# A decoder block on one Trainium2 core: other banks and delays in the mix, score sums on GpSimd, three feature tiles first, and gate and up by seven block products

## The chip, the core and the metric

The kernel runs on one core of a Trainium2 chip. The core has five engines with a queue each: TensorE (PE, matmuls; PEld is its weight load), VectorE (DVE), ScalarE (ACT), GpSimd (POOL) and SyncE (SP, which here issues DMAs). The metric is the device time of one execution in microseconds (us), the median of the runs shown. The profile shows one execution.

## The reference

One decoder block, 512 tokens of 1024 channels, all float32. Cut to its steps:

```python
xn = rms_norm(h, mix_norm)
attn_cols, rwkv_cols, gate_cols = split(xn @ w_in)
# per 128 queries: 8 heads of index scores, the best 128 keys are kept, attention over these
scores = einsum('bqhs,bqh->bqs', relu(q_idx @ k_idx.T * 64**-0.5), w_idx) * 8**-0.5
y_attn = softmax(q @ k_sel.T * scale + bias) @ v_sel        # q, k with an RMS norm per head
y_rwkv = rwkv7_time_mix(rwkv_cols)                          # a recurrence over the 512 tokens
merged = sigmoid(g_a) * (y_attn @ w_branch_attn) + sigmoid(g_r) * (y_rwkv @ w_branch_rwkv)
h = h + merged @ w_out
hn = rms_norm(h, ffn_norm)
gate, up = split(hn @ w_gate_up)                            # 1024 -> 2 x 2816
h = h + (silu(gate) * up) @ w_down                          # 2816 -> 1024
```

## The kernel before, in words

Large products are made of three float32r matmuls each: an operand is split into a high part and what is left, the low part (names end in h and l, or `hi` and `lo`), and high x high, high x low and low x high are summed in PSUM. Weights come as a stream of 129 tiles of 128x1024 in the order of use. `chunk` fetches one: SP issues the DMA into `w_raw` (L236), ACT makes `w_hi` (L239), and POOL subtracts to `w_lo` (L243); from tile 17 on (`POOL_ONLY`) every third `w_lo` is DVE's. There are 2, 3 and 3 buffers of the three.

**The mix** (0 to about 518 us): the norm, the projections of `w_in`, index scores, the search for the best 128 keys, attention, the RWKV recurrence in chunks of 64 tokens, and the gates. `scores` takes query blocks 1 to 3, with 256, 384 and 512 keys. For each of 8 heads TensorE makes the product, ACT the relu (L425), and DVE one multiply-and-add into `score` (L426). `select` then finds the best keys with MAX8 and MATCH_REPLACE8 on DVE (L438, L439). `split_heads` writes the high and low parts of q and k; `kl` is subtracted on DVE (L459). `matrices` makes the 128x512 products that the recurrence needs, in PSUM banks of the kind "i" (2 banks; "d" and "c" have 3 each).

**TensorE's order** is the order of the program. `Streams` makes it: each part of the work is a generator that yields how long (by the planner's own clock) it is to rest, and among those that are due the one with the lowest rank goes on; `products`, with all large matrix products, has the last rank and fills up. The rests are in the table `L` (L89). The order on the other engines is the scheduler's.

**After the mix**: `w_out` in matmuls of 256 columns (518 to 567), the second norm with its transposes (`norm`, L317 to L338: ACT squares, POOL `ss`, DVE `xs`, flips on TensorE, `hnh` on ACT, `hnl` on DVE), then **gate/up** in 22 feature tiles of 128: weights 128x128 of gate, then of up, are stationary and 512 tokens move, 2 x 8 x 3 = 48 matmuls. The first tile runs in halves of 256 tokens (`dense_halves`), so that it can begin before the last tokens are normalized. ACT makes the silu (L1096), DVE multiplies (L1097), ACT and POOL split the result into `uh` and `ul` (L1100, L1101), which stay in SBUF. **Down** goes twice over the 22 tiles, for 512 output channels each, in matmuls of 512 columns: 528 of them.

Of the kernel before, what the change touches and what calls it, by code (L numbers as in the profile page):

```python
# [127 lines left out]
def hybrid_block(ctx: ExitStack, tc: tile.TileContext, x, first, rows, consts, lora, rel_bias, stream, out):  # L128
# [324 lines left out]
    def split_heads(j, src, gain, hi, lo, twice):  # L453

        for e in range(2):
            a, b, h = slice(64 * e, 64 * e + 64), slice(64 - 64 * e, 128 - 64 * e), 2 * j + e
            if gain is None:
                nc.scalar.activation(hi[a, h], src[a], AF.Copy)
                nc.vector.tensor_sub(lo[b, h], src[a], hi[a, h])  # L459
            else:  # L460
# [285 lines left out]
    def matrices():  # L746
        yield "prep"
        for t in range(NT):
            if t > 1:
                yield f"inv{t - 2}"  # L750
                yield f"step{t - 2}"
            l16 = l16s[t % 2]
            for e in range(2):
# [226 lines left out]
    def products(wt, w2):  # L980
# [106 lines left out]
        for j in range(NF):
            wg, wu = w_tile(128), w_tile(128)
            ps, pu = bank("d"), bank("d")
            if j == 0:  # L1090
# [6 lines left out]
            nc.vector.tensor_mul(g, pu, g)  # L1097
            uh = fp.tile([128, S], F32R, name="uh", tag="uh", bufs=NF)
            ul = fp.tile([128, S], F32R, name="ul", tag="ul", bufs=NF)
            nc.scalar.activation(uh, g, AF.Copy)  # L1100
            nc.gpsimd.tensor_sub(ul, g, uh)  # L1101
            up.append((uh, ul))
# [110 lines left out]
```

## Time and profile before

| | |
|---|---|
| time, median of 3 runs | 939.4 us (937.67 to 939.57) |
| the profiled execution, its own time | 937.07 us |
| its span on the core | 934.9 us, so 2.2 us lie around it |
| TensorE busy | 97% of the span |
| DVE, ACT, POOL busy | 44%, 37%, 39% |
| mix; w_out and norm; gate/up; down | to about 518; to 576; 576 to 811; 811 to 931 us |
| HBM | 74.5 MB read, 82 GB/s over the span |

The page of the profile gives busy times of the whole span, which mix stages of different kinds, so the stages are read apart: from the waits of TensorE, from windows, and from the starts of single instructions. A matmul's recorded length is longer than its share of the pipeline; its price is the distance between the starts of successive ones. Some matmul records are missing, so counts may fall short by a few per cent.

### The profile page before, as it was taken

The numbers are of one execution on the slowest core, as the hardware profiler recorded it, in microseconds if no ns is written. First come the engines' busy times: TensorE is split into PE (matmuls) and PEld (weight loads), VectorE is DVE, ScalarE is ACT, GpSimd is POOL, SyncE is SP. The second block draws the span as 40 slices with busy tenths as digits, with TensorE's granted clock in tenths as the row PEclk, the third lists the DMA queues.
The fourth block names the chain that finished last, engine by engine and source line by source line (L and its number), as shares of the span: only waits on it lengthen the run. The fifth ranks groups of instructions, "written<-read, shape, count | busy, mean of one in ns | idle before, by whom it ended". The sixth has DMA issues, their size and how long they took to land.

```text
span 934.9 us, 13570 instructions
## 1 busy us (share of the span) xinstructions
PE 906.9 (97%) x5526; PEld 763.2 (82%) x5526; DVE 412.5 (44%) x796; ACT 344.0 (37%) x548; POOL 363.7 (39%) x242
## 2 busy tenths in 40 slices
PE   7999988999999999999999999999999999999998
PEld 5978986888687787878888998888888888888886
DVE  4399998874686457666334435111111111110111
ACT  5464665554543333333243225223222322311220
POOL 6425631313374344253236522544444353433321
PEclk9999999999999999999999999999999999999999
DMA  6312332111221110010432321333333323322431
GB/s 234 95 56 68 109 98 69 32 37 57 68 83 54 64 50 24 24 43 28 135 103 81 111 91 55 104 107 94 93 90 102 102 90 111 92 90 90 152 97 45
DMA packets 24173, 77.77 MB, mean 83 GB/s; under 512 B 2869, under 2 KB 4366, under 8 KB 24112
## 3 DMA queue, kind: packets, MB, share of 16 engines
q1 hardware_dynamic: 20688, 72.49, 24.8%
q10 hardware_dynamic: 3424, 4.43, 1.6%
q8 instruction: 43, 0.70, 0.3%
q14 instruction: 18, 0.15, 0.1%
HBM read 74.53 MB, written 2.38 MB: 82 GB/s over the span
## 4 chain that ended last, share of the span: by engine, by line
PE 84%; DVE 11%; issue 2%; ACT 2%; POOL 1%; DMA 1%; SPq 0%; DVEq 0%; ACTq 0%; POOLq 0%
PE ps_d L162 60%; PE ps_c L162 11%; PE ps_i L162 9%; DVE score L439 2%; DVE max L438 2%; PE ps_c L169 2%; DVE kl L459 1%; POOL w_lo L243 1%; DMA xa<-in_x_dram 1%; DVE score L426 1%; DVE lg L569 0%; PE ps_i L169 0%; DVE w_lo L243 0%; ACT lg L576 0%; PE ps_d L169 0%
## 5 line engine op out<-in xcount | busy, mean ns | idle before, releaser
L243 POOL TENSOR_TENSOR w_lo<-w_raw,w_hi 128x1024 fp32r<-128x1024 f32 (+1 forms) x94 | 223.5, 2379 | 355.0 <-ACT w_hi L239 328.8
L239 ACT ACTIVATE w_hi<-w_raw 128x1024 fp32r<-128x1024 f32 x129 | 136.7, 1060 | 351.6 <-PE ps_d L162 216.7
L162 PE MATMUL ps_d<-xnl,w_hi 128*128 128x512 f32 (+2 forms) x360 | 141.8, 394 | 0.0
L162 PE MATMUL ps_d<-xnh,w_hi 128*128 128x512 f32 (+2 forms) x360 | 141.4, 393 | 0.0
L162 PE MATMUL ps_d<-xnh,w_lo 128*128 128x512 f32 (+2 forms) x360 | 141.0, 392 | 0.0
L162 PE MATMUL ps_d<-hnl,w_hi 128*128 128x512 f32 (+1 forms) x368 | 139.9, 380 | 0.4 <-DVE hnl L338 0.4
L162 PE MATMUL ps_d<-hnh,w_hi 128*128 128x512 f32 (+1 forms) x368 | 139.8, 380 | 0.0
L162 PE MATMUL ps_d<-hnh,w_lo 128*128 128x512 f32 (+1 forms) x368 | 139.8, 380 | 0.0
L243 DVE TENSOR_TENSOR w_lo<-w_raw,w_hi 128x1024 fp32r<-128x1024 f32 x37 | 47.5, 1283 | 127.2 <-ACT w_hi L239 126.7
L1097 DVE TENSOR_TENSOR gsig<-ps_d,gsig 128x512 f32<-128x512 f32 x22 | 15.2, 692 | 157.6 <-PE ps_d L162 156.9
L162 PEld LDWEIGHTS ps_d<-hnl,w_hi 128*128 128x128 f32 x368 | 69.2, 188 | 13.8 <-DVE hnl L338 0.6
L162 PEld LDWEIGHTS ps_d<-hnh,w_lo 128*128 128x128 f32 x368 | 69.2, 188 | 13.1
L162 PEld LDWEIGHTS ps_d<-hnh,w_hi 128*128 128x128 f32 x368 | 69.2, 188 | 13.0
L162 PEld LDWEIGHTS ps_d<-xnh,w_hi 128*128 128x128 f32 x360 | 68.7, 191 | 11.7 <-issue 1.0
L162 PEld LDWEIGHTS ps_d<-xnl,w_hi 128*128 128x128 f32 x360 | 68.8, 191 | 11.2 <-issue 1.8
L162 PEld LDWEIGHTS ps_d<-xnh,w_lo 128*128 128x128 f32 x360 | 68.7, 191 | 11.2 <-issue 1.4
L1101 POOL TENSOR_TENSOR ul<-gsig,uh 128x512 fp32r<-128x512 f32 x22 | 31.5, 1433 | 25.3 <-ACT uh L1100 14.4
L162 PE MATMUL ps_d<-w_hi,mh 128*128 128x256 f32 x120 | 34.0, 284 | 0.0
L162 PE MATMUL ps_d<-w_hi,ml 128*128 128x256 f32 x120 | 34.0, 283 | 0.0
L162 PE MATMUL ps_d<-w_lo,mh 128*128 128x256 f32 x120 | 34.0, 283 | 0.0
L576 ACT ACTIVATE lg<-lg,mx,qrs 128x128 f32<-128x128 f32 (+3 forms) x32 | 20.8, 650 | 22.7 <-DVE mx L575 22.7
L438 DVE MAX8 max<-score 128x8 f32<-128x256 f32 (+2 forms) x48 | 26.7, 559 | 1.0
(291 smaller groups left out, 1685.7 us busy)
## 6 DMA issues: line engine op xcount, KB each, us to landing
w_raw<-in_stream_dram SPq DMA_DIRECT2D x129, 512.0 KB, 3.6
xa<-in_x_dram SPq DMA_DIRECT2D x4, 512.0 KB, 5.8
ht<-in_x_dram ACTq DMA_DIRECT2D x8, 256.0 KB, 5.9
out_dram<-ht SPq DMA_DIRECT2D x8, 256.0 KB, 2.1
toep<-bias_table ACTq DMA_DIRECT2D x8, 128.0 KB, 2.8
gain<-in_rows_dram ACTq DMA_DIRECT2D x2, 256.0 KB, 4.4
con<-in_consts_dram SPq DMA_DIRECT2D x1, 321.0 KB, 6.8
bias_table<-tab ACTq DMA_DIRECT2D x1, 276.0 KB
```

What stands on the lines that cost most here:

```text
L162: nc.tensor.matmul(o, w, r, **kw)
L169: nc.tensor.transpose(o, src, idn)
L239: nc.scalar.activation(hi, raw, AF.Copy)
L243: eng.tensor_sub(lo[:, o:o + n_], raw[:, o:o + n_], hi[:, o:o + n_])
L426: nc.vector.scalar_tensor_tensor(sc, r, w, sc, op0=OP.mult, op1=OP.add)
L438: nc.vector.max(m8, sc)
L439: nc.vector.match_replace(sc, m8, sc, TAKEN)
L459: nc.vector.tensor_sub(lo[b, h], src[a], hi[a, h])
L576: nc.scalar.activation(lg, lg, AF.Exp, scale=scale, bias=mx[:, 2:3], accum_out=den[:, h:h + 1])
L1097: nc.vector.tensor_mul(g, pu, g)
L1101: nc.gpsimd.tensor_sub(ul, g, uh)
```

## The change

**In the table of rests**: `score` from 0.4 to 0.6, `rms` 6.5 to 9.0, `attn` (0.9, 0.9, 0.95, 1.0) to (1.3, 1.1, 1.0, 1.0), with 0.7 more after the first two heads of a query block, `inv_u` 3.25 to 4.2. `matrices` takes its banks from the kind "d".

**Scores**: heads 0 to 4 stay as they are. Heads 5 to 7 are weighted and summed on POOL, and DVE adds that sum once per block. `kl` of `split_heads` goes to POOL.

**Three feature tiles first**: the first gate, the first up and the second gate weight tile run in the halves.

**Gate and up by seven products**: from the third feature tile on, the 2x2 blocks are gate and up by the two halves of the 1024 input channels (a11, a12, a21, a22) on the one side, and the two halves of channels by two halves of the tokens on the other (b11 and so on, and their differences t1 to t4). Winograd's form of Strassen's algorithm needs seven block products instead of eight, each 4 x 3 matmuls of 256 columns. `seven_sides` makes t1 to t4 once, from `hnh` + `hnl`. Each tile's s1 to s4 are made of the raw weights on DVE, and seven operands are split: high parts on ACT, low parts on DVE, except those of a12 and a22 on POOL. The product's result stays whole (`u`), and down splits it into `us` at use, in each of its two passes, on ACT and DVE.

```diff
-L = dict(norm=3.0, normed=1.3, score=0.4, pick=0.15, rms=6.5, sums=4.0, attn=(0.9, 0.9, 0.95, 1.0), attn_out=2.0, sig=0.3,
-         prep=5.0, oper=6.0, bonus=9.0, mat=0.5, mats=2.8, inv_u=3.25, inv_t=1.4, inv_r=1.4, inv_n=0.9, inv_e=1.8,
+L = dict(norm=3.0, normed=1.3, score=0.6, pick=0.15, rms=9.0, sums=4.0, attn=(1.3, 1.1, 1.0, 1.0), attn_new=0.7, attn_out=2.0, sig=0.3,
+         prep=5.0, oper=6.0, bonus=9.0, mat=0.5, mats=2.8, inv_u=4.2, inv_t=1.4, inv_r=1.4, inv_n=0.9, inv_e=1.8,
...
-                    nc.vector.scalar_tensor_tensor(sc, r, w, sc, op0=OP.mult, op1=OP.add)
+                    if h < 5:
+                        nc.vector.scalar_tensor_tensor(sc, r, w, sc, op0=OP.mult, op1=OP.add)
+                    else:
+                        nc.gpsimd.tensor_scalar(r, r, w, None, op0=OP.mult)
+                        if h > 5:
+                            nc.gpsimd.tensor_add(r, r, more)
+                        more = r
                 yield L["score"]
+            nc.vector.tensor_add(sc, sc, more)
...
-                nc.vector.tensor_sub(lo[b, h], src[a], hi[a, h])
+                nc.gpsimd.tensor_sub(lo[b, h], src[a], hi[a, h])
...
-            yield L["attn"][i]
+            yield L["attn"][i] + (L["attn_new"] if u < len(units) and units[u][1] < 2 else 0.0)
...
-                    ps = bank("i").rearrange("q (h t) -> q h t", h=4)
+                    ps = bank("d").rearrange("q (h t) -> q h t", h=4)
...
-                yield from dense_halves([(ps, wg), (pu, wu)], hn, "hn")
+                outs = [(bank("d"), w_tile(128)) for _ in range(3)]
+                yield from dense_halves(outs, hn, "hn")
+                (ps, _), (pu, _), (ps_1, _) = outs
+                quads = seven_sides(fp, four_k, hn_)
...
+        def product(ps, hi, lo, b, first):
+            for k in range(4):
+                ks = slice(k * 128, k * 128 + 128)
+                xh, xl = b[k]
+                mm(ps, hi[:, ks], xh, start=first and k == 0, stop=False, skip_group_check=True)
+                mm(ps, hi[:, ks], xl, start=False, stop=False, skip_group_check=True)
+                mm(ps, lo[:, ks], xh, start=False, stop=k == 3, skip_group_check=True)
+
+        for j in range(2, NF):
...
+            a11, a12, a21, a22 = wg[:, 0:512], wg[:, 512:1024], wu[:, 0:512], wu[:, 512:1024]
+            s1, s2, s3, s4 = [unit("s") for _ in range(4)]
+            nc.vector.tensor_add(s1, a21, a22)
+            nc.vector.tensor_sub(s2, s1, a11)
+            nc.vector.tensor_sub(s3, a11, a21)
+            nc.vector.tensor_sub(s4, a12, s2)
...
+            w11, ws2 = two(a11, nc.vector, s2, nc.vector)
+            w12, ws3 = two(a12, nc.gpsimd, s3, nc.vector)
+            ws1, w22 = two(s1, nc.vector, a22, nc.gpsimd)
...
+            product(pa, *w11, b11, True)
+            nc.scalar.activation(u2, pa, AF.Copy)
+            yield 0.0
+            product(pb, *ws2, t2, True)
+            nc.vector.tensor_add(u2, pb, u2)
+            yield 0.0
+            product(pa, *w12, b21, False)
+            nc.scalar.activation(g[:, 0:256], pa, AF.Silu)
+            yield 0.0
+            product(pc_, *ws3, t3, True)
+            nc.vector.tensor_add(u3, pc_, u2)
+            yield 0.0
+            product(pd, *ws1, t1, True)
+            nc.vector.tensor_add(u3, pd, u3)
+            yield 0.0
+            product(pc_, *w22, t4, False)
+            nc.vector.tensor_add(c21, pc_, u2)
+            yield 0.0
+            product(pd, *ws4, b22, False)
+            nc.vector.tensor_add(u2, pd, u2)
+            nc.scalar.activation(g[:, 256:512], u2, AF.Silu)
+            u = up_rows(j)
+            nc.vector.tensor_mul(u[:, 0:256], g[:, 0:256], c21)
+            nc.vector.tensor_mul(u[:, 256:512], g[:, 256:512], u3)
...
+                for k in range(2):
+                    s = fp.tile([128, 2, S], F32R, name="us", tag="fx", bufs=3)
+                    nc.scalar.activation(s[:, 0], up[k0 // 2][:, k], AF.Copy)
+                    nc.vector.tensor_sub(s[:, 1], up[k0 // 2][:, k], s[:, 0])
+                    uu.append(s)
```

In `seven_sides` a difference is two 512 subtractions (`tf`), a high part `th` on ACT and a low part `tl` on DVE, each 128x1024:

```diff
+            nc.vector.tensor_add(f[q], a[0][q // 2][:, s], a[1][q // 2][:, s])
...
+        d1, t1 = minus(block(0, 1), block(0, 0))
+        d2, t2 = minus(block(1, 1), d1)
+        _, t3 = minus(block(1, 1), block(0, 1))
+        _, t4 = minus(block(1, 0), d2)
```

What the scheduler makes of it is seen in three places. In the gate/up loop DVE had two kinds of instructions, multiplications and some of the `w_lo`:

```order
L243 TENSOR_TENSOR w_lo<-w_raw,w_hi 128x1024
L1097 TENSOR_TENSOR gsig<-ps_d,gsig 128x512 x2
L243 TENSOR_TENSOR w_lo<-w_raw,w_hi 128x1024
L1097 TENSOR_TENSOR gsig<-ps_d,gsig 128x512
L243 TENSOR_TENSOR w_lo<-w_raw,w_hi 128x1024
```

Now a tile has 16, of which these are the first twelve from the sum behind the second product on (L1137 to L1140 are s1 to s4 of the next tile, L1144 are low parts, the others are sums with PSUM):

```order
L1164 TENSOR_TENSOR post<-ps_d,post 128x256
L1144 TENSOR_TENSOR w_lo<-w_raw,w_hi 128x512
L1137 TENSOR_TENSOR s<-wu_raw 128x512
L1138 TENSOR_TENSOR s<-s,w_raw 128x512
L1139 TENSOR_TENSOR s<-w_raw,wu_raw 128x512
L1170 TENSOR_TENSOR post<-ps_c,post 128x256
L1140 TENSOR_TENSOR s<-w_raw,s 128x512
L1144 TENSOR_TENSOR w_lo<-s,w_hi 128x512
L1173 TENSOR_TENSOR post<-ps_i,post 128x256
L1144 TENSOR_TENSOR w_lo<-s,w_hi 128x512
L1144 TENSOR_TENSOR s4l<-s,s4h 128x512
L1176 TENSOR_TENSOR upt<-ps_c,post 128x256
```

The weights of the next tile are prepared between the sums of the running one. On DVE behind the last `hnl` stood a `w_lo` and the first multiplications; now `seven_sides` stands there (`hnf` is `hnh` + `hnl`, `tf` and `tl` belong to t1 to t4):

```order
L338 TENSOR_TENSOR hnl<-ps_c,hnh 128x4x128 x2
L1214 TENSOR_TENSOR hnf<-hnh,hnl 128x1024 x4
L1223 TENSOR_TENSOR tf<-hnf 128x512 x2
L1223 TENSOR_TENSOR tf<-hnf,tf 128x512
L1223 TENSOR_TENSOR tf<-hnf 128x512 x2
L1223 TENSOR_TENSOR tf<-hnf,tf 128x512 x2
L243 TENSOR_TENSOR w_lo<-w_raw,w_hi 128x1024
L1226 TENSOR_TENSOR tl<-tf,th 128x1024
L1223 TENSOR_TENSOR tf<-hnf,tf 128x512
L1115 TENSOR_TENSOR u<-ps_d,gsig 128x512
L1226 TENSOR_TENSOR tl<-tf,th 128x1024
L1144 TENSOR_TENSOR w_lo<-w_raw,w_hi 128x512
```

The sides of the products stand ahead of the fourth weight tile's multiplication and of the first low parts of the third feature tile. On POOL during the scores, before and then now (`relu` holds a head's weighted score):

```order
L243 TENSOR_TENSOR w_lo<-w_raw,w_hi 128x1024 x10
L486 TENSOR_TENSOR qrs<-qss,half 128x32
L243 TENSOR_TENSOR w_lo<-w_raw,w_hi 128x1024
L502 TENSOR_TENSOR qrs<-qss,half 128x8
L243 TENSOR_TENSOR w_lo<-w_raw,w_hi 128x1024
```

```order
L243 TENSOR_TENSOR w_lo<-w_raw,w_hi 128x1024 x6
L430 TENSOR_SCALAR relu<-relu,widx 128x256 x3
L432 TENSOR_TENSOR relu<-relu 128x256 x2
L243 TENSOR_TENSOR w_lo<-w_raw,w_hi 128x1024
L430 TENSOR_SCALAR relu<-relu,widx 128x384 x2
L243 TENSOR_TENSOR w_lo<-w_raw,w_hi 128x1024
L432 TENSOR_TENSOR relu<-relu 128x384
L430 TENSOR_SCALAR relu<-relu,widx 128x384
L432 TENSOR_TENSOR relu<-relu 128x384
L430 TENSOR_SCALAR relu<-relu,widx 128x512 x3
L432 TENSOR_TENSOR relu<-relu 128x512
L243 TENSOR_TENSOR w_lo<-w_raw,w_hi 128x1024
```

The four last `w_lo` of that row of ten now stand among the weighted scores and their sums.

## Rows read from the trace of the kernel before

**Rows 1.** The page's first part: busy time, share of the span and instructions of each engine.

```profile
PE 906.9 (97%) x5526; PEld 763.2 (82%) x5526; DVE 412.5 (44%) x796; ACT 344.0 (37%) x548; POOL 363.7 (39%) x242
```

**Rows 2.** TensorE's waits over the whole span: the waiting line, what it waited for, us in total, times, the longest.

```profile
PE ps_c L169 <- ACT lg L576: 6.2, 6, 2.3
...
PE ps_i L169 <- ACT ksq L503: 2.2, 1, 2.2
PE ps_c L162 <- DVE score L422: 1.9, 1, 1.9
PE ps_i L162 <- DVE uu L816: 1.8, 2, 1.1
PE ps_i L162 <- ACT tt L813: 1.6, 2, 1.1
PE ps_c L169 <- DVE xs L330: 1.2, 1, 1.2
```

**Rows 3.** Windows: from:to, length, busy time (and instructions) of PE, PEld, DVE, ACT, POOL, the granted clock of TensorE as a share of full speed, the DMA share, GB/s.

```profile
60.00:70.00 10.00, 8.10 (x29) 6.18 (x28) 9.76 (x21) 5.16 (x9) 3.07 (x2) 0.83 0.15 52
130.00:150.00 20.00, 17.41 (x101) 14.49 (x100) 19.02 (x48) 9.22 (x21) 4.77 (x2) 0.91 0.26 80
...
600.00:780.00 180.00, 180.00 (x796) 149.05 (x795) 25.24 (x28) 52.77 (x68) 75.41 (x39) 1.00 0.32 97
811.00:931.00 120.00, 120.00 (x530) 99.07 (x528) 12.89 (x14) 21.79 (x21) 34.74 (x15) 1.00 0.30 93
```

**Rows 4.** The timeline of TensorE in `w_out` (256 columns, the first and the last of 28 in a row) and in gate/up (512 columns, the first and the last of 10): start, recorded length, instruction.

```profile
529.74 0.28 PE L162 MATMUL ps_d<-w_hi,ml 128*128 128x256 f32 x1
...
532.98 0.28 PE L162 MATMUL ps_d<-w_hi,ml 128*128 128x256 f32 x1
...
595.41 0.39 PE L162 MATMUL ps_d<-hnh,w_lo 128*128 128x512 f32 x1
...
597.45 0.39 PE L162 MATMUL ps_d<-hnh,w_lo 128*128 128x512 f32 x1
```

**Rows 5.** The timeline of DVE and POOL where instructions of both meet, and once where POOL's is alone (803.83): start, length, instruction, idle time before it and its releaser.

```profile
120.73 2.23 DVE L459 TENSOR_TENSOR kl<-kraw,kh 64x512 fp32r<-64x512 f32 x1
...
120.06 2.35 POOL L243 TENSOR_TENSOR w_lo<-w_raw,w_hi 128x1024 fp32r<-128x1024 f32 x1 [0.28 <-ACT w_hi L239]
...
503.35 1.67 POOL L1067 TENSOR_TENSOR gr<-gr,mrg 128x512 f32<-128x512 f32 x1 [1.43 <-DVE gr L973]
...
503.79 2.31 DVE L243 TENSOR_TENSOR w_lo<-w_raw,w_hi 128x1024 fp32r<-128x1024 f32 x1
...
506.63 0.68 DVE L1069 SCALAR_TENSOR_TENSOR ml<-gr,mh 128x512 fp32r<-128x512 f32 x1
...
569.82 2.39 POOL L243 TENSOR_TENSOR w_lo<-w_raw,w_hi 128x1024 fp32r<-128x1024 f32 x1
...
570.71 1.29 DVE L338 TENSOR_TENSOR hnl<-ps_c,hnh 128x512 fp32r<-128x512 f32 x2 [0.83 <-ACT hnh L337]
...
594.71 1.23 DVE L243 TENSOR_TENSOR w_lo<-w_raw,w_hi 128x1024 fp32r<-128x1024 f32 x1 [0.15 <-ACT w_hi L239]
...
595.30 1.78 POOL L1101 TENSOR_TENSOR ul<-gsig,uh 128x512 fp32r<-128x512 f32 x1 [3.59 <-ACT uh L1100]
...
803.83 1.27 POOL L1101 TENSOR_TENSOR ul<-gsig,uh 128x512 fp32r<-128x512 f32 x1
```

**Rows 6.** Groups of instructions by line and form, from 567 to 931 us, and of the whole span for the 256 form of `ht`: busy time, mean ns of one, idle time before them and its releaser.

```profile
L243 DVE TENSOR_TENSOR w_lo<-w_raw,w_hi 128x1024 fp32r<-128x1024 f32 x21 | 25.7, 1225 | 116.7 <-ACT w_hi L239 116.2
...
L338 DVE TENSOR_TENSOR hnl<-ps_c,hnh 128x512 fp32r<-128x512 f32 x6 | 4.0, 688 | 1.6 <-ACT hnh L337 1.5
...
L1077 DVE TENSOR_TENSOR ht<-ps_d,ht 128x256 f32<-128x256 f32 x15 | 5.8, 420 | 18.9 <-PE ps_d L162 18.9
...
L243 POOL TENSOR_TENSOR w_lo<-w_raw,w_hi 128x1024 fp32r<-128x1024 f32 x44 | 105.3, 2393 | 190.6 <-ACT w_hi L239 190.6
...
L239 ACT ACTIVATE w_hi<-w_raw 128x1024 fp32r<-128x1024 f32 x65 | 68.9, 1061 | 249.1 <-PE ps_d L162 138.9 <-PE ps_i L162 82.9 <-issue 27.3
L1100 ACT ACTIVATE uh<-gsig 128x512 fp32r<-128x512 f32 x22 | 13.9, 632 | 0.0
L1096 ACT ACTIVATE gsig<-ps_d 128x512 f32<-128x512 f32 x22 | 12.8, 583 | 0.0
```

**Rows 7.** The timeline of DVE at the start of gate/up: the last two `hnl` and the first multiplication.

```profile
574.88 1.42 DVE L338 TENSOR_TENSOR hnl<-ps_c,hnh 128x512 fp32r<-128x512 f32 x2 [0.71 <-ACT hnh L337]
...
582.96 0.69 DVE L1097 TENSOR_TENSOR gsig<-ps_d,gsig 128x512 f32<-128x512 f32 x1 [0.70 <-ACT gsig L1096]
```

**Rows 8.** Groups by line and form: DVE from 40 to 150 us, and a POOL group of the whole span.

```profile
L459 DVE TENSOR_TENSOR kl<-kraw,kh 64x512 fp32r<-64x512 f32 x8 | 7.5, 933 | 0.2
...
L426 DVE SCALAR_TENSOR_TENSOR score<-relu,widx,score 128x384 f32<-128x384 f32 x7 | 5.8, 824 | 0.0
L426 DVE SCALAR_TENSOR_TENSOR score<-relu,widx,score 128x512 f32<-128x512 f32 x7 | 5.5, 782 | 0.0
...
L426 DVE SCALAR_TENSOR_TENSOR score<-relu,widx,score 128x256 f32<-128x256 f32 x7 | 4.1, 584 | 1.0 <-DVE score L426 0.5
...
L859 POOL TENSOR_TENSOR kbs<-kb,pchunk 128x512 f32<-128x512 f32 x7 | 7.3, 1037 | 0.4
```

More of the change, by code (lines that the diff above doesn't have):

```diff
@@ L33 @@
 UNITS, WBUFS = {"ua": 10, "uc": 8}, (2, 3, 3)
-UA = ("score", "relu", "widx_t", "tab", "ytile", "sg", "ag", "wa2", "seg", "am", "u32", "ht")
+UA = ("score", "relu", "widx_t", "tab", "ytile", "sg", "ag", "wa2", "seg", "am", "u32", "ht", "upt")
 SMALL = {"ss": 4, "max8": 3, "mx": 4}
@@ L1085, in products, with up_rows @@
         fp = ctx.enter_context(tc.tile_pool(name="ffn", bufs=1))
+        four_k = lambda name, tag, n: fp.tile([128, 4, 256], F32R if tag == "tx" else F32, name=name, tag=tag, bufs=n)
+        tags = ["d", "c", "i", "d", "c", "d", "c", "i"]
         up = []
-        for j in range(NF):
-            wg, wu = w_tile(128), w_tile(128)
-            ps, pu = bank("d"), bank("d")
+        def up_rows(j):
+            if j % 2 == 0:
+                up.append(fp.tile([128, 2, S], F32, name="u", tag="u", bufs=NF // 2))
+            return up[j // 2][:, j % 2]
@@ L1090, in products @@
+        for j in range(2):
             if j == 0:
-                yield from dense_halves([(ps, wg), (pu, wu)], hn, "hn")
-            else:
-                yield from dense_t(ps, wg, slice(0, 128), hn)
-                yield from dense_t(pu, wu, slice(0, 128), hn)
+                outs = [(bank("d"), w_tile(128)) for _ in range(3)]
+                yield from dense_halves(outs, hn, "hn")
+                (ps, _), (pu, _), (ps_1, _) = outs
+                quads = seven_sides(fp, four_k, hn_)
+            else:
+                ps, pu = ps_1, bank("d")
+                yield from dense_t(pu, w_tile(128), slice(0, 128), hn)
@@ L1095, in products @@
             g = unit("gsig")
             nc.scalar.activation(g, ps, AF.Silu)
[L1097 to L1102, printed above, removed]
+            nc.vector.tensor_mul(up_rows(j), pu, g)
+        b11, b21, b22, t1, t2, t3, t4 = quads
+        def product(ps, hi, lo, b, first):
[5 more added lines that the diff above has]
+                mm(ps, lo[:, ks], xh, start=False, stop=k == 3, skip_group_check=True)
@@ new lines, in products, with split, two @@
+        for j in range(2, NF):
+            wg = wp.tile([128, 1024], F32, name="w_raw", tag="w_raw", bufs=WBUFS[0])
+            wu = fp.tile([128, 1024], F32, name="wu_raw", tag="fx", bufs=3)
+            for w in (wg, wu):
+                nc.sync.dma_start(w, stream[at[0]])
+                at[0] += 1
+            a11, a12, a21, a22 = wg[:, 0:512], wg[:, 512:1024], wu[:, 0:512], wu[:, 512:1024]
[4 more added lines that the diff above has]
+            nc.vector.tensor_sub(s4, a12, s2)
+            def split(h, l, w, eng):
+                nc.scalar.activation(h, w, AF.Copy)
+                eng.tensor_sub(l, w, h)
+                return h, l
+            def two(wa, ea, wb, eb):
+                h = wp.tile([128, 1024], F32R, name="w_hi", tag="w_hi", bufs=WBUFS[1])
+                l = wp.tile([128, 1024], F32R, name="w_lo", tag="w_lo", bufs=WBUFS[2])
+                return split(h[:, 0:512], l[:, 0:512], wa, ea), split(h[:, 512:1024], l[:, 512:1024], wb, eb)
+            w11, ws2 = two(a11, nc.vector, s2, nc.vector)
+            w12, ws3 = two(a12, nc.gpsimd, s3, nc.vector)
+            ws1, w22 = two(s1, nc.vector, a22, nc.gpsimd)
+            ws4 = split(fp.tile([128, 512], F32R, name="s4h", tag="s4h", bufs=2),
+                        fp.tile([128, 512], F32R, name="s4l", tag="s4l", bufs=2), s4, nc.vector)
+            pa, pb, pc_, pd = [bank(tags[(4 * j + i) % 8])[:, 0:256] for i in range(4)]
+            post, upt, g = unit("post"), unit("upt"), unit("gsig")
+            u2, u3, c21 = post[:, 0:256], post[:, 256:512], upt[:, 0:256]
+            product(pa, *w11, b11, True)
[22 more added lines that the diff above has]
+            nc.vector.tensor_mul(u[:, 256:512], g[:, 256:512], u3)
@@ L1108, in products @@
                 wt = chunk(2, 512)
+                uu = []
+                for k in range(2):
[3 more added lines that the diff above has]
+                    uu.append(s)
                 last = k0 == NF - 2
@@ L1112, in products @@
                     j, ts = k0 + k, slice(t * 128, t * 128 + 128)
-                    uh, ul = up[j][0][:, ts], up[j][1][:, ts]
+                    uh, ul = uu[k][:, 0, ts], uu[k][:, 1, ts]
                     mm(pss[t], uh, wt[k][0], start=(j == 0), stop=False)
@@ L1119, in products, with seven_sides, block, minus @@
                         nc.sync.dma_start(out[t * 128:(t + 1) * 128, cs], ht[t][g])
+    def seven_sides(fp, four_k, a):
+        f = []
+        for q in range(4):
+            f.append(fp.tile([128, 2, S], F32, name="hnf", tag="u", bufs=NF // 2))
+            s = slice(2 * (q % 2), 2 * (q % 2) + 2)
+            nc.vector.tensor_add(f[q], a[0][q // 2][:, s], a[1][q // 2][:, s])
+        def block(k, t):
+            return [f[2 * k + e][:, :, 256 * t:256 * t + 256] for e in range(2)]
+        def minus(x, y):
+            d = four_k("tf", "u", NF // 2)
+            r = [d[:, 2 * e:2 * e + 2] for e in range(2)]
+            for e in range(2):
+                nc.vector.tensor_sub(r[e], x[e], y[e])
+            h, l = four_k("th", "tx", 8), four_k("tl", "tx", 8)
+            nc.scalar.activation(h, d, AF.Copy)
+            nc.vector.tensor_sub(l, d, h)
+            return r, [(h[:, k], l[:, k]) for k in range(4)]
+        d1, t1 = minus(block(0, 1), block(0, 0))
+        d2, t2 = minus(block(1, 1), d1)
+        _, t3 = minus(block(1, 1), block(0, 1))
+        _, t4 = minus(block(1, 0), d2)
+        as_is = lambda k, t: [(a[0][k][:, i, 256 * t:256 * t + 256], a[1][k][:, i, 256 * t:256 * t + 256])
+                              for i in range(4)]
+        return as_is(0, 0), as_is(1, 0), as_is(1, 1), t1, t2, t3, t4
     st.add(2, bias_table(), 30.0)
```

## The prediction

> **What bounds the kernel now.** I read the page's busy times first [rows 1]: TensorE is busy 97% of the span, so the time is what TensorE executes plus some thirty microseconds in which it waits or runs at a lower clock. Then TensorE's waits [rows 2]: nearly all lie in the mix, the longest sum (6.2 us) behind the softmax's `lg`, and in gate/up and down there is none but the 1.2 us for the last norm. So gate/up shortens only if TensorE gets fewer or shorter instructions, and the mix only by its waits. The windows [rows 3] add the clock: it is 0.83 in 60:70 and 0.91 in 130:150, 1.00 in gate/up and down.
>
> The price of a matmul is read from the starts of successive ones [rows 4]: at 256 columns 27 steps take 3.24 us, 120.0 ns each; at 512 columns 9 steps take 2.04 us, 226.7 ns each. Both kinds load new weights every time. Half the columns cost 53%, not 50%.
>
> **Gate/up on TensorE.** A feature tile took 2 x 8 x 3 = 48 matmuls of 512 columns: 10.88 us. With seven block products it takes 7 x 4 x 3 = 84 of 256: 10.08 us. That is -0.80 us for each of 20 tiles, **-16.0 us**. The third and fourth weight tile in the norm's halves: only one more (24 matmuls of 512, 5.44 us, become 48 of 256, 5.76 us), **+0.3 us**. The norm's 1.2 us wait stays, since the flips and what POOL has queued before `ss` are the same.
>
> Both prices lie 13.3 ns above the columns at 2.4 GHz (106.7 and 213.3 ns), and that fixed part takes a third of what fewer columns would give (84 x 106.7 against 48 x 213.3 ns would be -1.28 a tile). The Trainium skill ("TensorE: Matmul & The Clock Gate", section "Back-to-back issue gap") gives columns / 2.4 GHz plus about 2.5 ns. By that, 84 x 109.2 ns against 48 x 215.8 ns would be -1.2 us a tile and -24 us in all, and the sum 916 instead of 924. The trace does not agree (it shows 120.0 and 226.7), and the rows decide.
>
> **What the loop asks of DVE.** This is the term that decides. Gate/up now gives DVE 25.2 us in 180 [rows 3], 1.5 a tile; the new loop gives it 16 instructions: nine of 512 columns with both inputs in SBUF (s1 to s4 and five low parts), five of 256 with an input in PSUM, two multiplications of 256. Nine cost 0.69 us each alone, 0.60 when they follow at once (single ones 0.68 and 0.69, the pair of `hnl` 1.29 for two [rows 5, 6]). The 256 ones cost 0.42 [rows 6], less the same 0.09 when they follow at once, 0.33. So 5.4 + 2.3 = 7.7 to 6.2 + 2.9 = 9.1 us; I take 8.5, plus 0.5 for the last multiplication's wait on the second silu (ACT's 512 form takes 0.58 [rows 6]): 9.0 against TensorE's 10.08. It would fit, but POOL has two low parts of 512 a tile (a12, a22), 1.27 us each alone (the `ul` at 803.83 [rows 5]), and the two engines shut each other out. DVE's `w_lo` took 2.31 us instead of 1.22 when POOL's `gr` had begun before it, `kl` 2.23 behind POOL's `w_lo`; the other way, POOL's `ul` took 1.78 instead of 1.27 behind DVE's `w_lo` [rows 5]. DVE instructions that read PSUM pass: the `hnl` pair took 1.29 us with POOL's `w_lo` running [rows 5]. So a POOL instruction holds DVE between 0 (it falls beside the seven short instructions or the wait, some 2.8 of 9 us) and 1.27. I take 0.7, for DVE is mostly in the held kind: 9.0 + 1.4 = 10.4 us a tile. DVE then leads TensorE's 10.08 by 0.3, **+6 us** over 20 tiles; the range is 0 (DVE at or below 10.08) to +30 (9.1 + 2 x 1.27 = 11.6).
>
> ACT's ten copies and silus are 7 x 0.63 + 3 x 0.42 = 5.7 us of the tile, and POOL's two 2.5 to 3.6, so neither is the bound. Weight traffic is the same bytes in the same number of transfers.
>
> **The one-off start of the seven products.** After the last `hnl` (576.30 [rows 7]) DVE alone makes the sums and differences of the activations: four adds of 1024 at 1.22, eight subtractions of 512 at about 0.65, four low parts of 1024 at 1.22, one `w_lo` at 1.22, two multiplications at 0.69, then seven 512 ones of tile 2 up to the low part of s2: 4.9 + 5.2 + 4.9 + 1.2 + 1.4 + 4.6 = 22.2 us, to 598.5. TensorE wants that low part at 595.3: the first pair of tiles ended its halves just before the multiplication at 582.96 [rows 7], say 582.7; to it come 5.76 us of the third tile's halves, 5.44 of the fourth at 512, 1.44 of product 1. That is a stall of 3.2; holds by POOL add up to 2.5, a lower clock after it 1.7 at most, as in 60:70 (3.4 us at half speed). I take **+3.5**, 1.4 to 6.7.
>
> **Down.** The low and high parts of `u` are now made at use, once in each half of the columns. In 5.44 us of TensorE (24 matmuls) ACT has w_hi 1.06 and two copies of 0.63, DVE two subtractions of 0.69 and a third of the `w_lo`, POOL the rest at 2.39 [rows 6]. A chunk's parts need one chunk of lead, and TensorE ran without a break in 811:931 [rows 3]. At the turn between the halves four sums stand before a subtraction on DVE. **+0.5**, 0 to 1.5.
>
> **The mix.** DVE loses nine weightings of scores (a third of 21 in each width: 3 x (0.824 + 0.782 + 0.584) = 6.6 us), gains three adds (about 1.7), and loses eight `kl` (7.5 us): 12.4 us less [rows 8], in a stretch where it is 95 to 98% busy [rows 3]. POOL gains nine multiplications by a scalar and six adds; no row shows the first on POOL, the nearest is `kbs` at 1.04, the adds are as `ul` 1.27: (3 x 1.04 + 2 x 1.27) x (1 + 3/4 + 1/2) = 12.7 us, and eight `kl` of 512, 8.3 to 10.2. POOL has room (3.1 of 10 and 4.8 of 20 us busy [rows 3]), but its queue is in order: each `w_lo` that TensorE's projections need now stands behind sums that wait for ACT, and DVE's final add of a block waits for POOL's chain, with the search for the best keys of the block before (MAX8 and its replacing) queued behind it on DVE, and the softmax behind that. The longer delays and the other bank only move matmuls apart: they can remove waits, at most those named: 6.2 + 2.2 + 1.9 + 1.8 + 1.6 = 13.7 [rows 2], and the half-clock loss of 1.7 in 60:70 and 1.8 in 130:150. The select chain on DVE stays in sequence, and TensorE has to have other work to put between. I take half of 17, less 1.5 for new waits behind POOL: **-7**, from -15 to +4 (one `w_lo` held behind a block's 5.7 us of sums, and the clock after it).
>
> **Sum** against the profiled execution, 937.07 us (2.3 below the median of 939.4): -16.0 + 0.3 + 6 + 3.5 + 0.5 - 7 = -12.7, **924.4 us**; I say 924.
>
> **Rivals.** (a) TensorE is the bound throughout: DVE's holds fall beside short instructions, the mix's named waits go: 937.1 - 16.0 + 0.3 + 1.4 - 12.6 = 910. For it: 9.0 without holds fits under 10.08, and products of tile j+1 are prepared up to a tile ahead. Against: two holds a tile, and DVE's order is fixed. (b) DVE is the bound with about 10.9 a tile (1 us a hold): 20 x 0.8 = 16 us, which eats all of what TensorE gained: 934. (c) The mix's gain is eaten by POOL's queue: 0 instead of -7, 931, or 935 to 939 with the full +4 and a slower loop. (d) Slower: every POOL instruction holds DVE for its whole length and no DVE instruction follows at once, 9.1 + 2.5 = 11.6 us a tile, 1.5 above TensorE, 30 us instead of 6: 948. It decides from a DVE cycle of 11.0 on, where 20 x 0.93 equals the other gains. The rows of `w_lo` and `kl` speak for it, the pair of `hnl` beside POOL and the 0.60 against it.
>
> Rival (d) is also what the Trainium skill would say: "SBUF — State Buffer", section "SBUF: two separate sides", has the shared port pair as a lock that is held for the whole instruction, the loser blocked. The trace agrees for two SBUF inputs (2.31 against 1.22 us).
>
> **Chances.** Forecast 0.45 (918 to 930); (a) 0.20; (b) 0.15; (c) 0.08; (d) 0.12. The range 909 to 941 takes in all but most of (d) and the lower edge of (a). A difference under 0.2% (1.9 us) can't be told from none here. Faster: 0.45 + 0.20 + 0.14 + 0.05 = 0.84; same 0.05; slower 0.11.
>
> **What would show it.** In gate/up: starts 120.0 ns apart and TensorE's waits there. If the distance from tile to tile is 10.1 us, (a); if 10.3 to 10.6 with waits for `w_lo` or s4's parts from DVE, the forecast; 10.9 or more, (b) or (d), with DVE's 512 group near 1 us in the mean. One stall of 2 to 5 us near 595 to 599 shows the start. In the mix: the waits for `lg`, `score` and `uu` smaller, the clock near 1.0 at 60:70; new waits for POOL's `w_lo` mean (c). Down should stay at 120 us. It is wrong if the price at 256 columns isn't 120.0 ns in the loop, or if the mix moves by more than 15 us.

## The result, and the profile after

| | median, us | its ratio to before |
|---|---|---|
| before | 938.8 (937.67 to 939.57) | |
| changed kernel | 921.8 (921.08 to 923.69) | 0.9824 [0.9805, 0.9843] |

The change is faster by 1.8%. The profiled execution took 923.69 us with a span of 921.9, against 937.07 and 934.9 before; so the two traces are 13.0 us apart, the medians 17.0. Where the 13.0 come from is read from the chain of work that ended last (start, length, what). Of the kernel before, the wait ahead of the last norm and the first piece of down:

```profile
561.72 3.37 issue
...
811.36 2.04 PE ps_c L162 x9
```

The same two of the changed kernel, and two pieces between them:

```profile
544.19 3.37 issue
...
580.85 2.50 PE ps_c L162 x10
583.35 2.56 PE ps_d L162 x12
...
798.33 2.07 PE ps_c L162 x9
```

Up to the last norm the changed kernel is 17.5 us ahead (561.72 less 544.19). From there to down it took 254.1 us where the kernel before took 249.6: **gate/up became 4.5 us longer**. Down is as long as it was. So all of the gain, and more, came from the mix.

TensorE's waits now (compare [rows 2]):

```profile
PE ps_d L162 <- DVE post L1173: 5.2, 10, 0.7
...
PE ps_i L162 <- DVE post L1173: 4.7, 9, 0.5
...
PE ps_c L162 <- DVE w_lo L1144: 2.2, 1, 2.2
...
PE ps_d L162 <- ACT vt L1022: 0.6, 1, 0.6
PE ps_c L169 <- ACT lg L584: 0.5, 1, 0.5
PE ps_d L162 <- POOL w_lo L243: 0.5, 1, 0.5
...
PE ps_c L162 <- DVE score L422: 0.3, 1, 0.3
...
PE ps_i L162 <- ACT tt L821: 0.3, 1, 0.3
```

The mix's waits for `lg` (6.2), `ksq` (2.2), `score` (1.9), `uu` (1.8 in the longest line) and `tt` (1.6) are down to 1.1 in all; new ones, `vt` and `w_lo` the longest, stay under 1 us each. In gate/up there is a new one, 19 times for the sum L1173.

The windows (columns as in [rows 3]):

```profile
600.00:780.00 180.00, 170.96 (x1391) 167.51 (x1391) 166.28 (x267) 84.74 (x168) 55.05 (x34) 1.00 0.29 95
60.00:70.00 10.00, 9.65 (x47) 7.85 (x46) 9.66 (x26) 6.34 (x12) 8.27 (x6) 1.00 0.33 107
130.00:150.00 20.00, 20.00 (x111) 16.86 (x110) 16.96 (x49) 11.85 (x29) 5.07 (x2) 1.00 0.33 103
```

The clock at 60:70 and 130:150 went from 0.83 and 0.91 to 1.00; so did that of 390:400, which was 0.83. In gate/up TensorE, without a break before, is now idle 9 of 180 us, and DVE is busy 166 of 180.

One tile of the loop, first DVE and then POOL (timeline: start, length, instruction, idle time before it and its releaser):

```profile
671.87 0.42 DVE L1164 TENSOR_TENSOR post<-ps_c,post 128x256 f32<-128x256 f32 x1 [0.24 <-PE ps_c L162]
672.40 0.69 DVE L1144 TENSOR_TENSOR w_lo<-w_raw,w_hi 128x512 fp32r<-128x512 f32 x1
...
675.27 0.68 DVE L1140 TENSOR_TENSOR s<-w_raw,s 128x512 f32<-128x512 f32 x1
675.87 1.79 DVE L1144 TENSOR_TENSOR w_lo<-s,w_hi 128x512 fp32r<-128x512 f32 x1
677.58 0.41 DVE L1173 TENSOR_TENSOR post<-ps_d,post 128x256 f32<-128x256 f32 x1
```

```profile
675.34 1.77 POOL L1144 TENSOR_TENSOR w_lo<-w_raw,w_hi 128x512 fp32r<-128x512 f32 x1 [5.84 <-ACT w_hi L1143]
```

And TensorE at that place, the last matmul of the sixth product and the first three of the seventh:

```profile
677.23 0.28 PE L162 MATMUL ps_i<-th,w_lo 128*128 128x256 f32 x1
678.05 0.39 PE L162 MATMUL ps_d<-hnh,s4h 128*128 128x256 f32 x1 [0.54 <-DVE post L1173]
678.27 0.28 PE L162 MATMUL ps_d<-hnl,s4h 128*128 128x256 f32 x1
678.39 0.28 PE L162 MATMUL ps_d<-hnh,s4l 128*128 128x256 f32 x1
```

The seventh product is added onto the fifth in the same bank, and the sum L1173 must read the fifth alone first. L1173 stands behind the next tile's low part of s2, which POOL's low part of a12 held up (1.79 us instead of 0.68). TensorE waits with 0.82 us between two starts instead of 0.12, and its first matmul behind the wait takes 0.22: 0.70 + 0.10 = 0.8 us a tile. 10.08 + 0.8 is 10.9, and the tiles are 10.85 apart, as the starts of three successive seventh products show (chain of work):

```profile
667.20 1.69 PE ps_i L162 x12
...
678.05 1.70 PE ps_d L162 x12
...
688.91 1.69 PE ps_i L162 x12
```

### The profile page after: what moved, and what is told of

Read it like the earlier page. It is cut to its first block, busy times and chain, and to the rows that moved or that the text cites. A ratio compares the mean times of both kernels' runs of the same rounds, so it can differ in the third digit from the quotient of the medians.

```text
span 921.9 us, 15716 instructions
## 1 busy us (share of the span) xinstructions
PE 893.8 (97%) x6270; PEld 786.7 (85%) x6270; DVE 628.9 (68%) x1129; ACT 411.6 (45%) x714; POOL 366.4 (40%) x256
## 4 chain that ended last, share of the span: by engine, by line
PE 75%; DVE 7%; POOL 2%; issue 2%; ACT 2%; POOLq 0%; ACTq 0%; DVEq 0%
PE ps_d L162 41%; PE ps_c L162 18%; PE ps_i L162 14%; PE ps_c L169 2%; DVE w_lo L1144 1%; DVE post L1173 1%; DVE kr L716 1%; DVE sg L681 1%; POOL w_lo L243 1%; ACT w_hi L1143 1%; DVE tl L1226 1%; DVE hnf L1214 0%; DVE tf L1223 0%; POOL bb L710 0%; POOL ag L719 0%
## 5 line engine op out<-in xcount | busy, mean ns | idle before, releaser
L243 POOL TENSOR_TENSOR w_lo<-w_raw,w_hi 128x1024 fp32r<-128x1024 f32 (+1 forms) x67 | 158.7, 2371 | 201.7 <-ACT w_hi L239 194.6
L239 ACT ACTIVATE w_hi<-w_raw 128x1024 fp32r<-128x1024 f32 x89 | 93.9, 1055 | 111.1 <-PE ps_d L162 92.3
L1144 POOL TENSOR_TENSOR w_lo<-w_raw,w_hi 128x512 fp32r<-128x512 f32 x20 | 38.4, 1919 | 131.4 <-DVE post L1170 76.3
L1194 DVE TENSOR_TENSOR us<-u,us 128x512 fp32r<-128x512 f32 x44 | 36.6, 835 | 61.5 <-ACT us L1193 61.5
L162 PEld LDWEIGHTS ps_d<-xnh,w_hi 128*128 128x128 f32 x360 | 68.4, 190 | 10.7 <-issue 1.2
L1144 DVE TENSOR_TENSOR w_lo<-s,w_hi 128x512 fp32r<-128x512 f32 x60 | 75.4, 1258 | 0.1
L1144 POOL TENSOR_TENSOR w_lo<-wu_raw,w_hi 128x512 fp32r<-128x512 f32 x20 | 31.1, 1553 | 32.8 <-ACT w_hi L1143 32.8
L162 PE MATMUL ps_c<-w_hi,us 128*128 128x512 f32 x132 | 44.1, 389 | 0.0
L162 PE MATMUL ps_d<-w_hi,us 128*128 128x512 f32 x132 | 44.1, 389 | 0.0
L162 PE MATMUL ps_d<-hnl,w_hi 128*128 128x256 f32 (+1 forms) x136 | 40.0, 294 | 0.4 <-DVE hnl L338 0.4
L162 PE MATMUL ps_d<-hnh,w_hi 128*128 128x256 f32 (+1 forms) x136 | 39.9, 294 | 0.0
L162 PE MATMUL ps_d<-hnh,w_lo 128*128 128x256 f32 (+1 forms) x136 | 39.9, 294 | 0.0
```

The lines of the kernel that those rows point to most:

```text
L162: nc.tensor.matmul(o, w, r, **kw)
L239: nc.scalar.activation(hi, raw, AF.Copy)
L243: eng.tensor_sub(lo[:, o:o + n_], raw[:, o:o + n_], hi[:, o:o + n_])
L1144: eng.tensor_sub(l, w, h)
L1194: nc.vector.tensor_sub(s[:, 1], up[k0 // 2][:, k], s[:, 0])
```

## The experiments

The times of before beside the runs were 939.6 for the first four, 939.0 for e5 to e8, and 940.2 for the last two. Ratios are to before; the changed kernel's is 0.9824 [0.9805, 0.9843].

**Each half alone.** e1 has the new mix and the old gate/up and down, e2 the old mix and the new gate/up and down. In short, e1 against the changed kernel:

```diff
-        for j in range(2, NF):
-            wg = wp.tile([128, 1024], F32, name="w_raw", tag="w_raw", bufs=WBUFS[0])
+        for j in range(NF):
+            wg, wu = w_tile(128), w_tile(128)
...
```

and e2 against it:

```diff
-L = dict(norm=3.0, normed=1.3, score=0.6, pick=0.15, rms=9.0, sums=4.0, attn=(1.3, 1.1, 1.0, 1.0), attn_new=0.7, attn_out=2.0, sig=0.3,
+L = dict(norm=3.0, normed=1.3, score=0.4, pick=0.15, rms=6.5, sums=4.0, attn=(0.9, 0.9, 0.95, 1.0), attn_out=2.0, sig=0.3,
...
-                    ps = bank("d").rearrange("q (h t) -> q h t", h=4)
+                    ps = bank("i").rearrange("q (h t) -> q h t", h=4)
...
```

> The mix of the changed kernel (table of rests, bank, scores and kl on POOL) with gate/up and down of the kernel before. Theory A, the mix brought the whole gain and the seven products cost: the mix's 17.5 us alone, 938.8 - 17.5 = 921, between 918 and 923, as fast as the changed kernel or faster. Rival B, the gain came from gate/up as forecast and the mix brought about 7: near 932.

> The mix of the kernel before with three tiles first, the seven products and the new down. Theory A: slower than before by about 4.5 us, 943, with 10.85 us from tile to tile. Rival B (forecast): 6 us faster, 933.

Measured: e1 918.5 us, 0.9789 [0.9755, 0.9823]; e2 942.3 us, 1.0044 [1.0018, 1.0070]. Theory A holds and the forecast's split (B) is refuted: the mix brings about 20 us, and the seven products cost about 4. The two ratios multiply to 0.9832, the changed kernel's within its interval. In e2 the tiles are 10.86 us apart, as in the changed kernel. (e2's trace shows a granted clock of 0.95 in 620:770, but its starts within a product are 0.12 us apart, as at 1.00.) e1 was 3 us faster than the changed kernel, but the two intervals overlap; that e2 is slower than before is clear of the noise.

**What sets the cycle of the loop.** e3 gives the seventh product a bank of its own. That takes five banks a tile in turn where there were four, and one more sum on DVE; DVE's order from L1164 to L1173 is the same:

```diff
-            pa, pb, pc_, pd = [bank(tags[(4 * j + i) % 8])[:, 0:256] for i in range(4)]
+            pa, pb, pc_, pd, pe = [bank(tags[(5 * j + i) % 8])[:, 0:256] for i in range(5)]
...
-            product(pd, *ws4, b22, False)
+            product(pe, *ws4, b22, True)
             nc.vector.tensor_add(u2, pd, u2)
+            nc.vector.tensor_add(u2, pe, u2)
```

e4 leaves the bank and moves POOL's two low parts to DVE:

```diff
-            w12, ws3 = two(a12, nc.gpsimd, s3, nc.vector)
-            ws1, w22 = two(s1, nc.vector, a22, nc.gpsimd)
+            w12, ws3 = two(a12, nc.vector, s3, nc.vector)
+            ws1, w22 = two(s1, nc.vector, a22, nc.vector)
```

> The changed kernel, but the seventh product goes to a PSUM bank of its own instead of being added onto the fifth's, for one more 256 sum on DVE a tile; DVE's order stays. Theory C, the wait of the seventh product for the sum L1173, which must read the bank first, sets the cycle: the wait goes, 10.1 us a tile, some 14 us faster than the changed kernel, 908. Theory D, DVE's work with the holds by POOL sets it (10.1 us busy and 0.5 behind the silu of 10.85): the wait moves elsewhere, 10.9 us a tile and 922 to 925.

> The changed kernel with the low parts of a12 and a22 on DVE instead of POOL: DVE gets two more 512 instructions a tile (1.2 us at 0.60) and is not held any more (1.09 + 0.77 us in the tile at 667). Theory D: DVE needs 10.6 - 1.9 + 1.2 = 9.9 us, TensorE's 10.08 becomes the bound, 10.1 to 10.2 a tile, 908 to 910. Rival E, the holds overlap with waits and don't matter, the count of DVE instructions does: 11.4 to 12 a tile, 935 to 945.

Measured: e3 910.8 us, 0.9704 [0.9676, 0.9732]; e4 910.3 us, 0.9702 [0.9674, 0.9731]. Both are 11 us faster than the changed kernel. In e3 DVE has more to do than in the changed kernel, and the kernel is faster: theory D, as the bound of the changed kernel, falls. But e3's tiles come 10.31 us apart, not 10.08. Its DVE, from one tile's L1164 to the next (timeline):

```profile
665.78 0.43 DVE L1184 TENSOR_TENSOR u<-gsig,post 128x256 f32<-128x256 f32 x1 [0.49 <-ACT gsig L1181]
666.13 0.42 DVE L1164 TENSOR_TENSOR post<-ps_d,post 128x256 f32<-128x256 f32 x1
...
669.32 1.45 DVE L1140 TENSOR_TENSOR s<-w_raw,s 128x512 f32<-128x512 f32 x1
...
673.17 1.44 DVE L1144 TENSOR_TENSOR w_lo<-s,w_hi 128x512 fp32r<-128x512 f32 x1
...
676.10 0.43 DVE L1184 TENSOR_TENSOR u<-gsig,post 128x256 f32<-128x256 f32 x1 [0.48 <-ACT gsig L1181]
676.44 0.42 DVE L1164 TENSOR_TENSOR post<-ps_d,post 128x256 f32<-128x256 f32 x1
```

DVE waits only behind the silu (0.48) and is held twice by POOL (0.77 each, 1.45 against 0.68). So with the bank free DVE's work is the bound, 0.23 above TensorE. D was the next limit, not the first.

e4 is theory C once more, seen from the other side: its expectation of 10.1 to 10.2 under D was too low, the tiles are 10.36 apart (L1164 at 663.95 and 674.31). Its DVE and, in the second fence, TensorE:

```profile
663.95 0.42 DVE L1164 TENSOR_TENSOR post<-ps_c,post 128x256 f32<-128x256 f32 x1 [0.23 <-PE ps_c L162]
...
668.01 0.69 DVE L1144 TENSOR_TENSOR w_lo<-w_raw,w_hi 128x512 fp32r<-128x512 f32 x1
668.62 0.69 DVE L1144 TENSOR_TENSOR w_lo<-s,w_hi 128x512 fp32r<-128x512 f32 x1
669.22 0.42 DVE L1173 TENSOR_TENSOR post<-ps_d,post 128x256 f32<-128x256 f32 x1
...
674.31 0.42 DVE L1164 TENSOR_TENSOR post<-ps_d,post 128x256 f32<-128x256 f32 x1 [0.23 <-PE ps_d L162]
```

```profile
669.39 0.28 PE L162 MATMUL ps_i<-th,w_lo 128*128 128x256 f32 x1
669.69 0.39 PE L162 MATMUL ps_d<-hnh,s4h 128*128 128x256 f32 x1
```

L1173 ends at 669.64 and the seventh product starts at 669.69: it still waits for the bank, 0.18 us and the slow first matmul's 0.10. The chain from L1164 to L1173 lost the hold (1.79 to 0.69, 1.10) and gained the low part of a12 (0.61): 0.49 shorter by these lengths, 0.44 by the starts of the two sums (5.71 to 5.27), and the tile went from 10.85 to 10.36, by 0.49. DVE stands idle 0.23 before L1164. The cycle is that chain, from the second product over the nine DVE instructions L1164 to L1173 to the seventh product, and e4 accounts for it to a few hundredths of a microsecond.

**The one-off start.** The changed kernel runs two feature tiles in the old way; what the title counts as three are weight tiles, those in the halves. e5 runs a third feature tile in the old way before the seven products begin:

```diff
-        for j in range(2):
+        for j in range(3):
...
-        for j in range(2, NF):
+        for j in range(3, NF):
```

> The changed kernel with three plain feature tiles ahead of the seven products instead of two, 19 tiles by seven products. Theory G, the first tile by seven products stands 2.4 us for the low part of s2 and then runs 27 matmuls at half clock (2.5 us) because DVE has not ended the sides: with 10.88 us more lead both go, and a tile costs the same either way (10.85 against 10.88), so 5 us faster than the changed kernel, 916 to 918. Rival H, the stall is of the first tile itself and moves with it: no difference, 922.

Measured: 917.7 us, 0.9774 [0.9753, 0.9794], 4.1 us faster than the changed kernel and the tiles still 10.86 apart. Theory G holds. In the changed kernel TensorE stood for the low part of s2, 2.48 us between two starts:

```profile
578.36 0.28 PE L162 MATMUL ps_c<-tl,w_hi 128*128 128x256 f32 x1
580.85 0.58 PE L162 MATMUL ps_c<-th,w_lo 128*128 128x256 f32 x1 [2.21 <-DVE w_lo L1144]
```

Then it ran at 0.51 of its clock, in the window 580:586:

```profile
580.00:586.00 6.00, 5.15 (x24) 5.16 (x25) 4.56 (x9) 1.32 (x3) 0.00 (x0) 0.51 0.52 175
```

27 starts from there on are 0.21 us apart instead of 0.12, which costs 2.5 us of the start's 6.1 (the first tile by seven products had its seventh product 14.71 us after its first matmul, where 72 steps of 0.12 are 8.64). The other three runs of the changed kernel have a mean clock of 0.997 to 0.998 over the span against 0.996 in this one, so a part of the 2.5 is this run's own, and the medians are only 4.1 apart.

**The parts of the mix.** All three go back from e1 (918.5): e6 the bank, e7 heads 5 to 7 and `kl` to DVE, e8 the rests.

```diff
-                    ps = bank("d").rearrange("q (h t) -> q h t", h=4)
+                    ps = bank("i").rearrange("q (h t) -> q h t", h=4)
```

```diff
-                    if h < 5:
+                    if h < 8:
...
-            nc.vector.tensor_add(sc, sc, more)
...
-                nc.gpsimd.tensor_sub(lo[b, h], src[a], hi[a, h])
+                nc.vector.tensor_sub(lo[b, h], src[a], hi[a, h])
```

```diff
-L = dict(norm=3.0, normed=1.3, score=0.6, pick=0.15, rms=9.0, sums=4.0, attn=(1.3, 1.1, 1.0, 1.0), attn_new=0.7, attn_out=2.0, sig=0.3,
+L = dict(norm=3.0, normed=1.3, score=0.4, pick=0.15, rms=6.5, sums=4.0, attn=(0.9, 0.9, 0.95, 1.0), attn_new=0.0, attn_out=2.0, sig=0.3,
...
```

> The new mix alone (918.5), with the matrices' bank back to the kind i. Theory J, each of the three parts of the mix's change removes waits of its own stage, and the bank those of the recurrence (uu, tt, am: 4.5 us and a lower clock at 390): 2 to 6 us slower than the new mix alone, 920 to 925. Rival K, the longer rests alone bring it and the bank nothing: 918.5.

> The new mix alone with heads 5 to 7 and kl back on DVE; the rests and the bank stay new. Theory J: the waits for score and ksq return (4 us) and the lower clock at 60:70 and 130:150 (3.5 us): 4 to 8 us slower, 922 to 927. Rival K: 918.5, for the longer rests cover the later scores.

> The new mix alone with the old rests; bank, scores and kl stay new. Theory J: the waits for lg (6.2 us) and a part of those for uu and tt return: 6 to 10 us slower, 925 to 929. Rival K: all of the mix's gain goes, 935 to 940.

Measured: e6 921.3 us, 0.9819 [0.9791, 0.9848]; e7 923.6, 0.9836 [0.9819, 0.9853]; e8 926.7, 0.9866 [0.9847, 0.9885]. This fits theory J: by the medians the parts have shares of 2.7, 5.1 and 8.2, 16.0 of e1's 20 us; what becomes of the other 4 is not shown. The intervals separate e8 from e1; that of e7 overlaps e1's by a hair and e6's overlaps it widely, so for these two the waits have to carry the reading. e6's trace is its slowest run (925.3; the others 920.9 to 921.3), with a clock of 0.68 in 340:356 where e1 has 1.00, so only its waits are read here. Of the two below, e1 has 0.3 us, for `tt`. In e6:

```profile
PE ps_i L162 <- DVE uu L824: 1.6, 2, 0.8
...
PE ps_i L162 <- ACT tt L821: 0.8, 2, 0.5
```

In e7, the waits and the window 60:70, where the clock is back at 0.83 (over 66:74 it is 0.57, so some 3.4 of the 5.1 us are the clock's):

```profile
PE ps_c L162 <- DVE score L422: 2.2, 1, 2.2
PE ps_c L169 <- ACT lg L583: 1.4, 3, 0.7
```

```profile
60.00:70.00 10.00, 7.83 (x31) 6.23 (x29) 9.84 (x22) 5.42 (x9) 2.52 (x1) 0.83 0.28 95
```

In e8:

```profile
PE ps_c L169 <- ACT lg L584: 3.9, 4, 1.4
...
PE ps_d L162 <- POOL w_lo L243: 2.1, 1, 2.1
```

By the last line one `w_lo` comes 2.1 us too late once POOL has the score sums and the rests are the old ones. The wait ends at 95.75 us, and in 96:104 the clock is 0.57: another 3.4 us, more than the wait itself.

**All together.** e9 joins e3, e4 and e5, e10 joins e4 and e5 alone.

> The changed kernel with three plain tiles, a bank of its own for the seventh product, and the low parts of a12 and a22 on DVE. Theories C and D together: without the wait for the bank and without holds the next bound is DVE's work, 9.7 us and some wait behind the silu, or TensorE's 10.08: 10.1 to 10.2 us a tile, 903 to 906. Rival L, DVE's 19 instructions are the bound with the whole wait behind the silu: 10.3 to 10.4, 906 to 909.

> The same without the bank of its own: the sum L1173 is still read ahead of the seventh product, 10.36 us a tile as without POOL alone, and the start's 5 us less what a plain tile costs more (0.5): 910.3 - 4.5 = 906.

Measured: e9 **903.8 us**, 0.9626 [0.9592, 0.9659], 18 us below the changed kernel and 36 below before; e10 909.2 us, 0.9683 [0.9649, 0.9716]. In e9 the starts are 120.0 ns apart over the whole window and the tiles 10.08 us:

```profile
620.00:770.00 150.00, 150.00 (x1252) 150.00 (x1251) 142.73 (x285) 77.86 (x151) 0.00 (x0) 1.00 0.31 97
```

Rival L falls: the order that came out for DVE puts L1164 and a low part (here L1168 and L1148) into the wait behind the silu, so it is no loss any more. e10 gained less over e4 than expected, 1.1 us instead of 4.5; its tiles are 10.36 apart as forecast. One part of the difference lies in e4: its start stood for 2.0 us, but its clock stayed at 1.00 afterwards, so there was less to win. In the traces e10 is 2.6 us shorter from the first matmul of gate/up on (549.04 to 906.9 against 548.07 to 908.5), and its mix, the same program, is 1.0 longer; in seven traces with this mix that first matmul lies between 547.9 and 549.6. Why the clock fell in one kernel and not in the other is open, and the length of the stall doesn't tell: with 2.4 us it fell in e3 as well (0.72 in 580:586), but in e2 the starts behind the same 2.4 us are 0.12 apart.

## Why the prediction was right, and where it was not

The time came out as forecast (924, measured 921.8), but by luck: the loop and the start cost 10.7 us more than forecast, and the mix gave 10.5 more. By two of the forecast's own signs it was wrong: the mix moved by more than 15 us, and the tiles are 10.85 apart, not 10.3 to 10.6. By the terms of the sum, in the traces' 13.0 us:

- **TensorE's price**: 120.0 ns at 256 columns held in the loop, within a product every start is 0.12 us after the last. -16.0 + 0.3 was right. By the Trainium skill ("TensorE: Matmul & The Clock Gate", "Back-to-back issue gap"), whose formula the section gives for an isolated matmul, it would be 109 ns; the starts of e9's loop are 120.0 ns apart.
- **The loop on DVE**, forecast +6, measured +14.1: the 20 seventh products start between 591.10 and 796.72, 205.6 us where 19 x 10.08 are 191.5 (0.77 more a tile, less in the last ones; the first tile is counted with the start). The step that failed is "9.0 + 1.4 = 10.4 us a tile. DVE then leads TensorE's 10.08 by 0.3". The sum itself was nearly right: DVE is busy 166 of 180 us, 10.0 a tile, and waits 0.5 for the silu. But I added up durations and holds and compared engines, and did not follow which instruction of DVE's order TensorE waits for. The hold by POOL was there, 1.1 us on one low part; it cost so much since it stood in the chain L1164 to L1173 that the seventh product's bank waits for. e3 shows it: more work on DVE, no bank to wait for, 11 us less. Rival (b) gave nearly this cycle (10.9), but by the wrong mechanism.
- **The lock**: DVE's low part 1.79 us for 0.68 and POOL's 1.77 for 1.27. The Trainium skill's rule ("SBUF — State Buffer", "SBUF: two separate sides") holds here in both directions, and with POOL out of it (e4) every 512 instruction on DVE took 0.68 to 0.69. Rival (d), which would have needed two full holds a tile, 2.5 us, did not come: the two came to 1.1 and 0.8 us (the second low part took 1.44), and only the first lay in the chain. The sums with PSUM that ran beside a POOL instruction (L1176 here, L1170 in e3) took 0.41 and 0.42, so they are not held.
- **The start**, forecast +3.5, measured 2.4 of standing, 2.5 of lower clock, 0.5 before the first seventh product and 0.7 in shorter waits and the matmuls behind them: +6.1, inside the range, though the lower clock was taken as 1.7 at most. The stall came where it was placed, at the low part of s2 (580.8 after the last `hnl` at 558.8, 22 us later as summed; some 1.6 of them are holds by POOL, which the sum had apart).
- **Down**, forecast +0.5: 0.
- **The mix**, forecast -7, range -15 to +4, measured -17.5. The mechanism was right and the size not: the named waits and the clock came to 17, and I took half of it for want of a reason. Nearly all of it went: the named waits fell by 12.6, two smaller ones of the recurrence by 1.1, the clock gave 5.2 (1.7 of them in 390:400, which I had not counted), and new waits took 1.8, together 17.1. POOL's queue, which now works 8.3 of the 10 us in 60:70 instead of 3.1, let TensorE wait no more than half a microsecond for a `w_lo`. That TensorE had projections left to fill the longer rests is likely, but no run shows it apart.

-15.7 + 14.1 + 6.1 - 17.5 = -13.0, as between the spans. The changed kernel's second half is its weaker one: the old gate/up with the new mix (e1) is no slower, and the seven products pay once the bank's wait or POOL's hold is gone (e3 and e4 are 8 us below e1), and most with both gone and a third feature tile in the old way (e9).

## What to carry to other kernels

Where two engines are nearly balanced, the sums of their work don't give the cycle: follow one turn of the loop from a result back to the instruction that may reuse its buffer, in the order in which each queue stands. A partial sum that is read and then accumulated further in the same PSUM bank makes TensorE wait for the reader; a second bank and one more sum were worth 11 us here. When a change is made of halves, time each half alone: here one hid the loss of the other.

## What the runs showed of the hardware that I had not expected

A multiplication by a scalar per partition on POOL was dearer than the nearest row had let me think (1.04 us for 512), and dearer than POOL's sum of two tiles. By width in the changed kernel, where the means take in longer ones (the shortest of 512 and 384 took 1.56 and 1.25 us),

```profile
L430 POOL TENSOR_SCALAR relu<-relu,widx 128x512 f32<-128x512 f32 x3 | 5.0, 1691 | 1.8 <-ACT relu L425 1.8
L430 POOL TENSOR_SCALAR relu<-relu,widx 128x384 f32<-128x384 f32 x3 | 3.9, 1321 | 1.0 <-ACT relu L425 1.0
...
L432 POOL TENSOR_TENSOR relu<-relu 128x512 f32<-128x512 f32 x1 | 1.3, 1287 | 0.0
```

In the loop the first matmul behind a wait takes 0.22 us to the next start instead of 0.12 (in 18 of 19 waits, 0.19 in the other), so that each of these waits costs 0.10 us more than its length. After stalls of 2.0 and 2.4 us at the same place the clock stayed at 1.00 in one kernel (e4) and fell to 0.51 in the other. And at the start POOL's low part of a12 took 5.75 us (from 572.22): DVE ran six instructions with two SBUF inputs behind each other, and POOL's ended 1.2 us after the start of the next one, L1115, which reads PSUM (576.73).
